# One full-array product for two 64x64 ones in the chunked recurrence of a hybrid backbone

## The chip, the cores and the metric

The kernel runs on one core of a Trainium2 chip. The metric is the device time of one execution in microseconds; the number to forecast is the median over several runs. TensorE appears in the profile as PE (the products) and PEld (the loads of the stationary operand, which overlap PE), VectorE as DVE, ScalarE as ACT, GpSimd as POOL, and the engine that issues the transfers as SP.

## The reference

Two layers over 1024 latent tokens and 256 context tokens, width 1024, all in float32. Each layer mixes tokens with three head groups (a gated MLP, a windowed attention, and an RWKV-7 recurrence of 4 heads of 64, run forwards and backwards), then applies a SwiGLU. What matters here is the recurrence:

```
def update(S, w_t, k_t, v_t, kk_t, a_t):
    sa = jnp.einsum('bhvk,bhk->bhv', S, kk_t)
    return (S * w_t[:, :, None, :] - sa[..., None] * (kk_t * a_t)[:, :, None, :]
            + v_t[..., None] * k_t[:, :, None, :])
def step(S, x):
    S = update(S, *x[1:])
    return S, jnp.einsum('bhvk,bhk->bhv', S, x[0])
```

## The kernel before

The recurrence is computed by chunks of 64 tokens. A chain is one direction and one pair of heads: 4 chains, 5 groups of 4 chunks each, so 80 units (`ul`) per layer and 160 in the kernel. The two heads of a pair lie on partitions 0 to 63 and 64 to 127. For every chunk the inverse of a 64x64 triangular matrix is made beforehand and kept in DRAM (`tb`), the two heads' inverses one below the other.

A unit passes through four stages. `u0` forms two masked 128x128 products. `u1` multiplies each head's inverse (`Ti`, 64x64) by that head's half of `t`. `u4` makes two 128x128 products, one for each head. `u5` updates the state (a 128x64 stationary operand per head, tile `u`) and makes the output (tile `uy`). The loop over n calls, for each n, u5 of unit n-4, u0 of unit n, u4 of unit n-2 and u1 of unit n-1, and then some background work: the output stage `rw_out` of chains that have ended (tile `gg`), and loads and splits of coming weights. The order in which TensorE gets the instructions is set when the program is compiled, and it isn't always that of the code. Every float32 product appears in the trace as two loads and two matmuls; so a stage with two products shows four of each. All of them carry L147, the line of the helper `mm`, and are told apart by tiles: u0 reads `u<-bC,bC`, u1 `u<-U,bC`, u4 `u<-bC`, u5 `u<-bC,U`, the output `uy<-U,bC`.

Three sets of four SBUF slots (`CH`) hold the operands of a group by turns (group number modulo 3). `chunk_set` zeroes and fills what stays constant in them. `beta_load` issues the loads of a group two groups ahead: two of `AB` (L1187), `KR` (L1189), `Ti` (L1190), the values `ZV` (L1196). `Ti` and `ZV` lie in a slot of their own (`C3`), taken afresh for each group. PSUM has two banks for u0, two for u4 and one each for u1, u5, uy and the background.

Of the kernel before, what the change touches and what calls it, by code (L numbers as in the profile page):

```python
# [93 lines left out]
def trunk(ctx: ExitStack, tc: tile.TileContext, x, ctxt, cc, w_mod, pp, w_in, w_out, lng, lnb, sgw, sink,  # L94
          w2, a2, g2, w_gu, w_down, cst, rope, out, dbg=None):
    nc = tc.nc
    V, S, G, T, D = nc.vector, nc.scalar, nc.gpsimd, nc.tensor, nc.sync
# [14 lines left out]
    def alloc(name, dt=F32):  # L112
        i = free.popleft()
        return Slot(sp.tile([128, NTOK], dt, tag=f"s{i}", name=nm(name)), i)
# [14 lines left out]
    def p_t(tag, bufs, n=512):  # L129
        return psum["pool"].tile([128, n], F32, tag=tag, name=nm(tag), bufs=bufs)  # L130
# [15 lines left out]
    def mm(o, lhsT, rhs, start=True, stop=True, parts=False):  # L146
        T.matmul(o, lhsT=lhsT, rhs=rhs, start=start, stop=stop, skip_group_check=parts)  # L147
# [42 lines left out]
    def bg(n, lane=0):  # L190
        q = (bgq, elq)[lane]
        owed[lane] += n
        while owed[lane] >= 1 and q:
            try:
                owed[lane] -= next(q[0]) or 1
            except StopIteration:
                q.popleft()
        if not q:
            owed[lane] = 0.0
# [96 lines left out]
    AB = [cp.tile([128, 4, 16], F32, name=f"ab{l}") for l in range(L)]  # L296
# [236 lines left out]
    def layer(l):  # L533
# [28 lines left out]
        tb = dr.tile([4, 128, NTOK], F32, name=f"tb{l}")  # L562
# [316 lines left out]
        for name in ("v", "u"):  # L879
# [3 lines left out]
            for t0 in range(0 if full else 2, NT, 2):  # L883
# [10 lines left out]
                for j in range(2):  # L894
                    t = t0 + j
# [248 lines left out]
        CH = []  # L1144

        def chunk_set():

            CH.append([alloc("bC") for _ in range(4)])  # L1150
            (V if CS else G).memset(CH[-1][2].t[:, 0:1024], 0.0)
            yield
            G.tensor_copy(CH[-1][3].t[:, 512:576], I2)
            for z in range(2):
                hp = slice(64 * z, 64 * z + 64)
                cv = CH[-1][z].t[hp, 0:1024].rearrange("p (c w) -> p c w", w=128)
                if CS > z:
                    S.activation(cv[:, :, 64:128], I2[hp].unsqueeze(1).to_broadcast([64, 8, 64]), AF.Copy)
                else:
                    G.tensor_copy(cv[:, :, 64:128], I2[hp].unsqueeze(1).to_broadcast([64, 8, 64]))  # L1160
                yield
# [9 lines left out]
        def beta_load(ci, gi):  # L1171

            d, pair = chains[ci]
            while ("join", ci) not in rw:
                bg(1, 1)
            H0, H1, AB, KR = (z.t[:, 0:1024] for z in CH[gl.index((ci, gi)) % 3])
            C3 = alloc("bC3")
            noY = gi == 0 and not full
            ZV, Ti = C3.t[:, 0:512], C3.t[:, 512:768]
            grp[ci, gi] = dict(c0=64 if noY else 0, H=(H0, H1), AB=AB, KR=KR, Ti=Ti, pc=(ci * 5 + gi) * 4, ZV=ZV, sl=C3)  # L1180
            src = cb[ci, gi]

            def c8(ap, q):
                return ap.rearrange("p (c q) -> p c q", q=q)
            for h in range(2):
                hp = slice(64 * h, 64 * h + 64)
                D.dma_start(c8(AB[hp], 128)[:, :, 64 - 64 * h:128 - 64 * h], c8(src[hp, 0:512], 64))  # L1187
            nw = 1 if noY else 2
            D.dma_start(KR[:, 0:256 * nw], src[:, 512:512 + 256 * nw])  # L1189
            D.dma_start(Ti, tb[ci][:, gi * 256:(gi + 1) * 256])  # L1190
            for h, H in enumerate((H0, H1)):
                hp = slice(64 * h, 64 * h + 64)
                later.append((H[hp].rearrange("p (c w q) -> p w c q", w=2, q=128)[:, 0:nw, :, 0:64],
                              KR[hp, 0:256 * nw].rearrange("p (w c t) -> p w c t", w=nw, t=64)))
            vs = vt[d, gi * 256:gi * 256 + 256, pair * 128:(pair + 1) * 128]
            D.dma_start(ZV[0:64].rearrange("p (c f) -> p c f", f=128), vs.rearrange("(c t) f -> t c f", t=64))  # L1196
            if gi == 0:
                G.memset(ZV[64:128, 0:128], 0.0)


        def unit(ci, gi, c):
            m = (ci * 20 + gi * 4 + c) % (2 * len(UR))
            g = grp[ci, gi]
            return g, UR[m // 2].t[:, m % 2 * 640:m % 2 * 640 + 512], g["c0"], [z[:, c * 256:c * 256 + 256] for z in g["H"]]
# [16 lines left out]
        def u1(ci, gi, c):  # L1221
            g, t, c0, C = unit(ci, gi, c)
            p = p_t("u1", PB["u1"])
            for h in range(2):
                hp = slice(64 * h, 64 * h + 64)
                mm(p[hp, c0:128], g["Ti"][hp, c * 64:c * 64 + 64], t[hp, c0:128])
            for h in range(2):
                oh = slice(64 - 64 * h, 128 - 64 * h)
                S.activation(C[h][oh, 128 + c0:256], p[oh, c0:128], AF.Copy)
# [93 lines left out]
        ul = [(ci, gi, c) for ci in range(4) for gi in range(5) for c in range(4)]  # L1323
        gl = [(ci, gi) for ci in range(4) for gi in range(5)]
        stages = {0: u0, 1: u1, 4: u4, 5: u5}

        def beta_start():
            yield from chunk_set()
            beta_load(*gl[0])
            yield  # L1330
            yield from chunk_set()
            own()
            beta_load(*gl[1])
            for _ in range(4):
                yield
            own()
# [27 lines left out]
        ps_open(True)  # L1364
        rw["beta"] = True
        run(chunk_set())
        UR = [alloc("U") for _ in range(NU)]
        GB = {}
        for n in range(len(ul) + max(s[1] for s in LG)):
            if n % 4 == LD and n // 4 + 2 < len(gl):  # L1370
                beta_load(*gl[n // 4 + 2])
            if n % 4 == (LD + OL) % 4:
                own()
            for s, lag in LG:
                m = n - lag
                if 0 <= m < len(ul):
                    ci, gi, c = ul[m]
                    stages[s](ci, gi, c)
                    if s == 5 and chains[ci][0] == 1 and c == 3 and gi in (0, 2, 4) and (full or gi):
                        bgq.append(rw_out(chains[ci][1], {0: 0, 2: 2, 4: 1}[gi]))  # L1380
            if n >= len(ul) - 24 and n % 4 == 1 and len(ready) < WR:
                emit_w(len(ready) >= 1)
            if n == len(ul) - 12 or (full and n == len(ul) - 9):
                GB[len(GB)] = gb_tile(l, 0, len(GB))
            if n < len(ul) + 2:
                bg(2 if n >= len(ul) - 8 else 1)
            bg(EL_B, 1)
# [576 lines left out]
```

## Time and profile before

| | |
|---|---|
| median of 3 runs | 3276.86 us (3274.75 to 3278.19) |
| profiled execution | 3271.0 us, of which the span from first to last instruction is 3269.2 us |
| PE busy | 3153.1 us (96%) |
| DVE, ACT, POOL busy | 62%, 41%, 16% of the span |
| stretches with the recurrence | 590 to 780 us (first layer), 2285 to 2480 us (second layer) |

Busy time is the time in which an engine has an instruction in work; the ends of matmuls are modelled, so neighbouring matmuls overlap in it. How long a product holds TensorE is better read from the starts of the loads: from the first load of one product to the first load of the next. In a timeline a row stands for several instructions of one kind in a row (x4), with the start of the first and the time until the last has ended.

### The profile page before, as it was taken

The page shows a single profiled execution, that of the slowest core. Times are in us where ns is not written, and L with a number is a line of the kernel's source. Part 1 is how long each engine was busy: PE and PEld are TensorE (multiplying, and loading weights), DVE is VectorE, ACT ScalarE, POOL GpSimd, SP SyncE. Part 2 cuts the span into 40 slices and gives each one's busy share as a digit, 9 for nine tenths or more (in the row PEclk, how much of TensorE's full clock was granted, in tenths as well). Part 3 has the DMA queues.
Part 4 walks back from the last instruction along what each step waited for, and adds up shares of the span by engine and source line. Part 5 has one row for each costly group of instructions (what it writes and reads, how often), then busy time and mean ns, then how long its engine had stood idle before and what let it go on. Part 6 is the DMA issues. An engine that isn't in the chain of part 4 may idle for free.

```text
span 3269.2 us, 51898 instructions
## 1 busy us (share of the span) xinstructions
PE 3153.1 (96%) x19892; PEld 2568.1 (79%) x19892; DVE 2038.0 (62%) x3978; ACT 1349.4 (41%) x2805; POOL 538.5 (16%) x616
## 2 busy tenths in 40 slices
PE   7998999999999999999999998999999999999998
PEld 4777978777788888886688777877777788888887
DVE  3458869676475555554455657779676666666556
ACT  4354477665342222222112544377665433333211
POOL 2103101232112222210001203101122122231000
PEclk8898999999999999999999999999999999999999
DMA  5684321445621212235722375412445222223322
GB/s 216 213 263 145 103 59 55 128 132 193 210 67 59 73 63 71 71 114 201 268 86 78 105 237 173 139 56 79 120 127 200 85 78 78 91 78 135 96 104 97
DMA packets 395176, 403.96 MB, mean 124 GB/s; under 512 B 113456, under 2 KB 334640, under 8 KB 394928
## 3 DMA queue, kind: packets, MB, share of 16 engines
q1 hardware_dynamic: 394928, 400.64, 37.8%
q8 instruction: 157, 2.57, 0.3%
q14 instruction: 91, 0.75, 0.1%
HBM read 279.97 MB, written 120.59 MB: 123 GB/s over the span
## 4 chain that ended last, share of the span: by engine, by line
PE 80%; DVE 8%; DMA 3%; issue 3%; ACT 3%; POOL 2%; SPq 1%; DVEq 0%; POOLq 0%; ACTq 0%
PE dd L147 26%; PE mm L147 24%; PE xx L147 18%; PE u L147 7%; PE mm L1118 1%; DMA wraw<-in_w_mod 1%; PE gg L147 1%; PE uy L147 1%; PE xx L1118 1%; DVE eX L666 1%; DVE eL L664 1%; DVE P L1071 1%; POOL ss L179 0%; DMA wm<-in_w_mod 0%; DVE yac L1697 0%
## 5 line engine op out<-in xcount | busy, mean ns | idle before, releaser
L147 PE MATMUL mm<-h,wh 128*128 128x512 f32 (+1 forms) x1424 | 424.2, 382 | 2.9 <-ACT ntmp L399 2.3
L147 PE MATMUL mm<-wh,h 128*128 128x256 f32 x1472 | 327.3, 299 | 0.5 <-DVE rtmp L946 0.5
L147 PE MATMUL dd<-h,wh 128*128 128x256 f32 (+1 forms) x1312 | 321.8, 336 | 1.5 <-DVE h L407 1.0
L147 PEld LDWEIGHTS mm<-h,wh 128*128 128x128 f32 x1424 | 261.8, 193 | 59.4 <-issue 10.0
L147 PE MATMUL mm<-h,wl 128*128 128x512 f32 (+1 forms) x712 | 268.5, 377 | 1.1 <-DVE wl L232 1.1
L147 PEld LDWEIGHTS mm<-wh,h 128*128 128x128 f32 x1472 | 252.1, 197 | 16.9 <-issue 15.8
L147 PEld LDWEIGHTS dd<-h,wh 128*128 128x128 f32 x1312 | 228.0, 191 | 29.2 <-DVE h L407 1.2
L1575 ACT ACTIVATE wh<-wq 128x1024 fp32r<-128x1024 f32 x114 | 121.0, 1061 | 302.8 <-PE dd L147 113.9
L147 PE MATMUL dd<-h,wl 128*128 128x256 f32 (+1 forms) x656 | 219.3, 334 | 0.0
L147 PE MATMUL mm<-wl,h 128*128 128x256 f32 x736 | 213.2, 290 | 4.3 <-DVE wl L232 4.3
L1576 DVE TENSOR_TENSOR wl<-wq,wh 128x1024 fp32r<-128x1024 f32 x114 | 141.1, 1238 | 114.8 <-ACT wh L1575 114.8
L179 POOL TENSOR_TENSOR ss<-ss,mh_sb 128x1 f32<-128x1 f32 x74 | 50.5, 683 | 838.2 <-DVE ss L376 836.0
L147 PE MATMUL dd<-tt,wh 128*128 128x512 f32 x608 | 188.1, 391 | 0.0
L147 PEld LDWEIGHTS mm<-h,wl 128*128 128x128 f32 x712 | 136.8, 192 | 25.3 <-DVE wl L232 1.4
L1697 DVE TENSOR_TENSOR yac<-yac,mm 128x512 f32<-128x512 f32 x126 | 86.4, 686 | 109.2 <-PE mm L147 109.2
L147 PEld LDWEIGHTS mm<-wl,h 128*128 128x128 f32 x736 | 145.0, 197 | 7.4 <-DVE wl L232 4.7
L1697 DVE TENSOR_TENSOR yac<-yac,xx 128x512 f32<-128x512 f32 x126 | 86.3, 685 | 91.8 <-PE xx L147 91.7
L1565 POOL TENSOR_TENSOR wq<-wu 128x512 f32<-128x512 f32 x38 | 49.1, 1292 | 561.8 <-DVE wl L1576 477.8
L147 PEld LDWEIGHTS dd<-h,wl 128*128 128x128 f32 x656 | 124.9, 190 | 12.4
L147 PEld LDWEIGHTS dd<-tt,wh 128*128 128x128 f32 x608 | 111.7, 188 | 21.3
L147 PE MATMUL u<-bC,bC 128*128 128x128 f32 (+1 forms) x640 | 118.3, 303 | 0.3 <-DVE bC L1219 0.3
L147 PE MATMUL dd<-tt,wl 128*128 128x512 f32 x304 | 118.3, 389 | 0.0
(370 smaller groups left out, 7769.7 us busy)
## 6 DMA issues: line engine op xcount, KB each, us to landing
wm<-in_w_mod SPq DMA_DIRECT2D x80, 512.0 KB, 5.2
wr<-in_w_down SPq DMA_DIRECT2D x44, 512.0 KB, 4.6
wr<-in_w_in SPq DMA_DIRECT2D x38, 512.0 KB, 4.4
cb<-ao SPq DMA_DIRECT2D x76, 256.0 KB, 2.7
wu<-in_w_gu SPq DMA_DIRECT2D x38, 512.0 KB, 3.7
wq<-in_w_gu SPq DMA_DIRECT2D x38, 512.0 KB, 3.7
ao<-rk SPq DMA_DIRECT2D x58, 256.0 KB, 4.0
xs<-xr SPq DMA_DIRECT2D x28, 512.0 KB, 2.7
```

What stands on the lines that cost most here:

```text
L147: T.matmul(o, lhsT=lhsT, rhs=rhs, start=start, stop=stop, skip_group_check=parts)
L179: G.tensor_tensor(dst, src, mh[:, :n], op=ALU.pow)
L664: V.tensor_tensor(tmp, Lm[:, j + 1:, j:j + 1].to_broadcast([n, r, c]), X[:, j:j + 1, :c].to_broadcast([n, r, c]), op=ALU.mult)
L666: V.tensor_tensor(X[:, j + 1:, :c], X[:, j + 1:, :c], tmp, op=ALU.subtract)
L1071: V.tensor_tensor_reduce(out=po, in0=pi, in1=m, scale=1.0, scalar=-3.0e38, op0=ALU.add, op1=ALU.max, accum_out=mx[:, h:h + 1])
L1118: T.transpose(ps[:, z * 128:(z + 1) * 128], P[i // 2].t[:, c:c + 128], ident)
L1565: G.tensor_tensor(a[:, 0:512], u[:, 0:512], u[:, 512:1024], op=ALU.add)
L1575: S.activation(w.hi[i], raw[i], AF.Copy)
L1576: V.tensor_tensor(w.lo[i], raw[i], f32(w.hi[i]), op=ALU.subtract)
L1697: V.tensor_tensor(yac[t].t[:, c], yac[t].t[:, c], ps, op=ALU.add)
```

## The change

The two heads' inverses are put on the diagonal of a 128x128 square that is zero elsewhere. `Ti` moves from `C3` into free columns (640 to 1151) of the fourth slot of the group's set in `CH`, which `chunk_set` zeroes once. The loads of `Ti` write only the two diagonal blocks, in two transfers, one for each head, instead of one. `u1` is then one product over all 128 rows and columns instead of two with 64x64.

```diff
             G.tensor_copy(CH[-1][3].t[:, 512:576], I2)
+            G.memset(CH[-1][3].t[:, 640:1152], 0.0)
...
-            H0, H1, AB, KR = (z.t[:, 0:1024] for z in CH[gl.index((ci, gi)) % 3])
+            cset = CH[gl.index((ci, gi)) % 3]
+            H0, H1, AB, KR = (z.t[:, 0:1024] for z in cset)
             C3 = alloc("bC3")
             noY = gi == 0 and not full
-            ZV, Ti = C3.t[:, 0:512], C3.t[:, 512:768]
+            ZV, Ti = C3.t[:, 0:512], cset[3].t[:, 640:1152]
...
-            D.dma_start(Ti, tb[ci][:, gi * 256:(gi + 1) * 256])
+            for h in range(2):
+                hp = slice(64 * h, 64 * h + 64)
+                D.dma_start(c8(Ti[hp], 128)[:, :, 64 * h:64 * h + 64], c8(tb[ci][hp, gi * 256:(gi + 1) * 256], 64))
...
             p = p_t("u1", PB["u1"])
-            for h in range(2):
-                hp = slice(64 * h, 64 * h + 64)
-                mm(p[hp, c0:128], g["Ti"][hp, c * 64:c * 64 + 64], t[hp, c0:128])
+            mm(p[:, c0:128], g["Ti"][:, c * 128:c * 128 + 128], t[:, c0:128])
```

## Rows read from the trace of the kernel before

**Rows 1.** The page: busy time of the engines; shares of the chain that ended last.
```profile
PE 3153.1 (96%) x19892; PEld 2568.1 (79%) x19892; DVE 2038.0 (62%) x3978; ACT 1349.4 (41%) x2805; POOL 538.5 (16%) x616
PE 80%; DVE 8%; DMA 3%; issue 3%; ACT 3%; POOL 2%; SPq 1%; DVEq 0%; POOLq 0%; ACTq 0%
```
**Rows 2.** Windows: window, length, busy PE PEld DVE ACT POOL, clock, DMA share, GB/s.
```profile
590.00:780.00 190.00, 185.21 (x1866) 139.60 (x1863) 138.39 (x451) 132.22 (x454) 54.19 (x66) 1.00 0.49 144
2285.00:2480.00 195.00, 186.73 (x1826) 142.74 (x1825) 133.83 (x439) 130.27 (x444) 45.10 (x61) 0.99 0.45 130
```
**Rows 3.** Waits of PE, longest in each stretch: us in total, times, longest.
```profile
PE mm L147 <- POOL Y L1275: 1.3, 1, 1.3
...
PE mm L1118 <- ACT P L1093: 2.5, 2, 2.2
```
**Rows 4.** Timeline of weight loads, 612 to 614 us: one unit in program order.
```profile
612.18 0.52 PEld L147 LDWEIGHTS u<-bC,bC 128*128 128x128 f32 x4
612.62 0.53 PEld L147 LDWEIGHTS u<-bC 128*128 128x128 f32 x4
613.27 0.20 PEld L147 LDWEIGHTS u<-U,bC 64*64 64x64 f32 x4
613.63 0.20 PEld L147 LDWEIGHTS u<-bC,U 128*64 128x64 f32 x4 [0.17 <-issue]
...
614.02 0.52 PEld L147 LDWEIGHTS u<-bC,bC 128*128 128x128 f32 x4
```
**Rows 5.** Timeline of weight loads, 702 to 705 us: one unit in another order.
```profile
702.39 0.19 PEld L147 LDWEIGHTS u<-U,bC 64*64 64x64 f32 x4
702.76 0.30 PEld L147 LDWEIGHTS u<-bC,bC 128*128 128x128 f32 x2 [0.17 <-issue]
703.17 0.19 PEld L147 LDWEIGHTS uy<-U,bC 128*64 128x64 f32 x2
703.43 0.30 PEld L147 LDWEIGHTS u<-bC,bC 128*128 128x128 f32 x2
703.85 0.20 PEld L147 LDWEIGHTS u<-bC,U 128*64 128x64 f32 x4
...
704.23 0.52 PEld L147 LDWEIGHTS u<-bC 128*128 128x128 f32 x4
704.88 0.20 PEld L147 LDWEIGHTS u<-U,bC 64*64 64x64 f32 x4
```
**Rows 6.** Instructions of tile u, those of u1: ns min/median/max, first and last start, forms.
```profile
L147 PEld LDWEIGHTS u<-U,bC x640: 129/130/133, 592.7 to 2472.2; 64*64 64x64 f32 x160
L147 PE MATMUL u<-U,bC x640: 218/269/320, 592.7 to 2472.3; 64*64 64x128 f32 x144, 64*64 64x64 f32 x16
```
**Rows 7.** Windows, instructions on tile u alone: busy PE, PEld, DVE, ACT.
```profile
590.00:780.00 190.00, 150.28 (x1264) 110.53 (x1264) 107.74 (x396) 88.06 (x316) 1.00 0.49 144
```
**Rows 8.** Transfers of a group: issue ns by line, landing us, and SP's longest wait.
```profile
L1190 SPq DMA_DIRECT2D bC<-tb x40: 319/382/943, 513.5 to 2443.9; - x40
L1187 SPq DMA_DIRECT2D bC<-cb x80: 573/625/821, 563.7 to 2442.5; - x80
bC<-cb SPq DMA_DIRECT2D x84, 128.0 KB, 2.8
SPq L1187 <- PE u L147: 73.7, 15, 8.5
```
**Rows 9.** GpSimd's memset at line 544: ns min/median/max, first and last start.
```profile
L544 POOL MEMSET lora<- x2: 951/952/954, 24.2 to 1823.9; 128x1024 f32 x2
```
**Rows 10.** The chain in order of time, end of the first layer's recurrence.
```profile
770.79 0.27 ACT bC L1229
...
771.52 0.84 ACT mhi L1413
```

## The prediction

> **What bounds the kernel now.** I began with the page. PE is busy for 96% of the span and carries 80% of the chain that ended last [rows 1]; so time taken off TensorE should come off the end, unless another engine bounds the stretch in question. The change touches the recurrence alone, and I read its two stretches next. In both PE is busy for 186 to 187 us, where DVE and ACT have 130 to 138 us, and the granted clock is 1.00 and 0.99, the upper of its two levels (2.4 GHz) [rows 2]. PE hardly waits: the longest entry of its waits is 1.3 us in the first stretch and 2.5 us in the second [rows 3], and all of them together are 4.5 us (5 rows) and 7.5 us (11 rows). DVE has 107.74 us and ACT 88.06 us of work for the 80 units' tile u, 1.35 and 1.10 us a unit [rows 7], against at least 1.84 us in which a unit passes through PE [rows 4]. So the reader should look for what a unit costs on PE.
>
> The starts of the loads tell that. In [rows 4] the eight loads of u0 and u4 follow each other by 0.11 us (0.44 us for four). After u4's last load, though, 0.32 us go by until u1's first: u4 takes 0.65 us where its four loads alone explain 0.44. The shape changes there, from 128x128 to 64x64. The same extra stands in [rows 5] at the change to 128x64: the second half of u0, two loads, holds PE for 0.42 us (703.43 to 703.85), so 0.31 us from last load to next. I take 0.31 us for a step at which the shape changes away from 128x128, against 0.11 us where it stays. PE's "waits" don't show this time.
>
> **What the change removes and adds on PE.** Now u1 has four loads of 64x64, in pairs side by side, and the next product's first load comes 0.36 to 0.37 us after u1's first (613.27 to 613.63, 702.39 to 702.76). From u4's last load over u1 to whatever follows is thus 0.31 + 0.37 = 0.68 us. With the change u1 has two loads of 128x128 and no change of shape behind u4. No row shows such a u1, but u0 and u4 are the same instruction in form.
> - Where a 128x64 product follows (u5 or uy, as in [rows 4]), the three steps become 0.11 + 0.11 + 0.31 = 0.53 us: 0.15 us saved. The switch isn't lost, it moves behind u1.
> - Where a 128x128 product follows (half of u0 as in [rows 5], or background gg), they become 3 x 0.11 = 0.33 us: 0.35 us saved, because two switches go.
>
> The trace has 640 loads of u1 [rows 6], four for each of 160 units. By walking through all of them in the loads' timeline I count 84 of the first kind and 64 of the second; a dozen have other neighbours, or loads missing from the record, and I give them nothing. Sum: 84 x 0.15 + 64 x 0.35 = 12.6 + 22.4 = 35 us. Sixteen units have only 64 moving columns (the second form of the matmuls in [rows 6]); u1 is cheaper there already, and I take off 2 us as an estimate. That is the upper end with the order kept: 33 us.
>
> Then what isn't bound by PE. In the last stretch of each recurrence the chain runs through ACT, with u1's evacuation beside splits of the output stage [rows 10], about six units a layer. Twelve units at the mean saving of 0.22 us are 2.6 us that I strike, and 2.4 us more for places where PE's existing short waits [rows 3] grow because PE arrives earlier. 33 - 5 = 28 us.
>
> **What covers the rest.** *The second transfer.* Each of 40 groups gets two strided issues instead of one. They have the form of AB's, 0.625 us each against 0.382 us for Ti now [rows 8]: 2 x 0.625 - 0.382 = 0.87 us of SP a group, 35 us in all. SP has that time: it stands 73.7 us in the first layer at L1187 alone, waiting for PE to be through with a set [rows 8]. Behind Ti stand ZV and the background's loads. If the cover were gone, a group would start 0.87 us late, up to 35 us; I take nothing, for the reason that follows. *A new wait.* Ti now overwrites columns that u1 of three groups back still reads, so its issue waits for the last u1 of that group, with ZV behind it on SP. AB already waits for the u0 of the same unit, which PE passes one unit earlier, 1.84 to 2.49 us [rows 4, 5]; two issues of AB and one of KR, at 0.6 us each [rows 8], take up 1.8 us of that, so SP stops for another 0 to 1 us. Between that u1 and the first that reads the new Ti lie eight units, at least 8 x 1.84 = 14.7 us, and a load lands in 2.8 us [rows 8]; so below it is nothing, and above, with 1 us on each of 34 groups and no slack, 34 us. I take nothing. *The memsets.* Six on GpSimd, half the width of one that takes 0.952 us [rows 9], so at most 0.95 us and nearer 0.5; POOL is busy for 54 of 190 us [rows 2], and the first u1 that reads them comes later. The third set's could hold u0's operands up by 1 us a layer; I take nothing and keep 2 us for the range. *Evacuation.* L1229 reads the same PSUM tile as before. u1's first load comes 0.20 us sooner (0.31 - 0.11), its last one 0.11 us behind that, so the result isn't later and I charge nothing.
>
> Against the profiled execution of 3271.0 us (3269.2 us of span and 1.8 us around it) 28 us less is 3243.0 us. It lies 5.9 us below the median of the runs, so I forecast 3276.9 - 28 = 3249 us.
>
> **A rule that speaks against it.** The rows show that u1's two products run side by side: four loads of 0.13 us each end 0.19 to 0.20 us after the first began [rows 4, 5, 6]. Without the 0.20 us that the switch adds (0.31 - 0.11) a u1 costs 0.37 - 0.20 = 0.17 us now; a full one costs 2 x 0.11 = 0.22 us. Taken alone the product gets dearer by 0.05 us. The Trainium skill ("TensorE: Matmul & The Clock Gate", Part 3, on packing small matmuls) says just that: products of 64 rows and columns in separate quarters of the array run at the same time, and that is the remedy for small ones; the change undoes it. By that rule alone the kernel would be slower. The rows around u1 decide otherwise, because they show the switch as well, and the trace agrees with the packing but not with its being the cheaper form here.
>
> **The rivals.**
> 1. *Order gets worse* (other side). PE's order is set at compile time: the code has u5, uy, u0, u4, u1, yet [rows 5] have u0 split around uy. A unit in program order takes 1.84 us (612.18 to 614.02), one in the order of [rows 5] takes 2.49 us (702.39 to 704.88). With the change they take 1.69 and 2.14 us. Fewer products in u1 may make the planner place u0 and uy elsewhere. Each unit that goes from the first order to the second costs 0.45 us: at 62 units the 28 us are gone, at 90 units the time is 3276.9 + 12 = 3289 us. For it: 47 of the units already stand with u0 or uy split, by my count in the loads' timeline, and small things decide. Against it: the work to be ordered and the lags are the same.
> 2. *Order gets better*: the same in reverse, or more units with u0 next to u1. With two switches gone everywhere, 150 x 0.35 = 52 us, 3225 us.
> 3. *The switch stays*, and the pairs side by side were free: u1 lands between 128x64 products, or the step isn't one of shape at all. 160 x 0.05 = 8 us more, 3285 us. Against it: u0 to u4 has no such step.
> 4. *ACT becomes the bound*: a unit's ACT work with the output's evacuation and splits is near 1.3 us on average, 132.22 us in 190 us [rows 2], and comes in order. If half the savings fall on its waits, 14 us remain: 3263 us.
>
> **How the numbers follow.** Forecast 0.53 (3241 to 3257); worse order 0.15, of which 0.03 stay faster, 0.05 end level and 0.07 slower; better order 0.14; the switch stays 0.05, slower; ACT binds 0.13, of which 0.02 end level. A measurement can tell about 0.2%, 6.6 us, from no change. Faster: 0.53 + 0.03 + 0.14 + 0.11 = 0.81; same 0.07; slower 0.12. The range goes from the better order's 3225 up to a gain just lost, 3279: what is left out is the slower cases above it, 0.12, and little below.
>
> **What will show it.** Right: 320 loads of 128x128 for u1 in place of 640; 0.11 us between u4's last load and u1's first; 0.31 us from u1's last load to a u5; a unit in program order of about 1.69 us; recurrence stretches some 14 us shorter each, the rest unchanged. Wrong: more units with u0 split around uy; PE waits for L1229 or L1254 in the stretches; u1 at a group's start waiting for the transfer of tb; or a step of 0.3 us that still stands ahead of u1.

## The result and the profile after

The changed kernel takes 3299.52 us (median of 4 runs, 3297.27 to 3301.01) against 3277.51 us of the kernel before (4 runs of its own on the same chip): ratio 1.0068, 95% interval 1.0056 to 1.0080. It is 22 us slower where 28 us less was forecast, outside the range of 3225 to 3279. The profiled execution took 3301.01 us.

What the prediction said of the products themselves came true. The instructions on tile `u` (count, then ns min/median/max, first and last start, forms) answer to [rows 6]: half as many loads, all of them full.

```profile
L147 PEld LDWEIGHTS u<-U,bC x320: 186/192/333, 593.3 to 2498.8; 128*128 128x128 f32 x160
L147 PE MATMUL u<-U,bC x320: 222/275/421, 593.4 to 2498.9; 128*128 128x128 f32 x144, 128*128 128x64 f32 x16
```

The timeline of weight loads from 603.6 to 605.6 us (start, length, engine, line) shows a unit in program order, as [rows 4] did.

```profile
603.65 0.30 PEld L147 LDWEIGHTS u<-U,bC 128*128 128x128 f32 x2
604.07 0.20 PEld L147 LDWEIGHTS u<-bC,U 128*64 128x64 f32 x4
604.18 0.20 PEld L147 LDWEIGHTS uy<-U,bC 128*64 128x64 f32 x4
604.45 0.52 PEld L147 LDWEIGHTS u<-bC,bC 128*128 128x128 f32 x4
604.89 0.53 PEld L147 LDWEIGHTS u<-bC 128*128 128x128 f32 x4
605.34 0.30 PEld L147 LDWEIGHTS u<-U,bC 128*128 128x128 f32 x2
```

From one u1 to the next are 1.69 us (603.65 to 605.34), the very number forecast. u4's four loads and the step to u1 take 0.45 us instead of 0.65; the 0.42 us from u1 to u5 are 0.11 + 0.31, so the switch of shape has moved behind u1.

Yet the stretches got longer. From the first to the last load of the recurrence's products the first takes 190.4 us (591.5 to 781.9; before 183.0, 590.6 to 773.6), the second 187.0 us (2317.9 to 2505.0; before 179.4, 2298.7 to 2478.1). The page's line of busy time and its shares of the chain, for [rows 1] (this chain goes back over less than a third of the span, so its shares can't be set beside those of before):

```profile
PE 3160.0 (96%) x19572; PEld 2590.7 (79%) x19572; DVE 2037.4 (62%) x3978; ACT 1350.4 (41%) x2805; POOL 541.1 (16%) x622
PE 26%; issue 1%; DVE 1%; ACT 1%; POOL 0%; DMA 0%; POOLq 0%; DVEq 0%; ACTq 0%
```

Windows over the two stretches, columns as in [rows 2], and PE's longest waits from 590 to 795 us, as in [rows 3] (L1256 and L1231 are L1254 and L1229 of before; the two waits of tile `dd` lie behind the stretch):

```profile
590.00:780.00 190.00, 179.99 (x1690) 147.13 (x1685) 129.47 (x437) 123.53 (x437) 51.42 (x64) 0.99 0.45 127
2300.00:2510.00 210.00, 191.24 (x1721) 154.71 (x1720) 139.47 (x452) 133.76 (x453) 46.62 (x62) 0.96 0.43 119
```

```profile
PE u L147 <- ACT bC L1256: 2.8, 5, 1.2
PE dd L147 <- DVE mlo L1416: 1.7, 1, 1.7
PE dd L147 <- ACT mhi L1415: 1.5, 1, 1.5
PE uy L147 <- ACT Yb L1269: 1.4, 1, 1.4
PE u L147 <- ACT bC L1231: 1.2, 3, 0.7
```

PE is now idle for 10.0 us of the first window (190.00 - 179.99), where it was for 4.8. No single wait explains it. What does is seen in the timeline of weight loads a little later, over four units from the u1 at 617.79 to that at 626.04 us:

```profile
617.79 0.30 PEld L147 LDWEIGHTS u<-U,bC 128*128 128x128 f32 x2
618.01 0.68 PEld L147 LDWEIGHTS u<-bC,bC 128*128 128x128 f32 x4
...
619.22 0.30 PEld L147 LDWEIGHTS u<-U,bC 128*128 128x128 f32 x2
...
620.02 0.30 PEld L147 LDWEIGHTS u<-bC,bC 128*128 128x128 f32 x2
...
620.69 0.30 PEld L147 LDWEIGHTS u<-U,bC 128*128 128x128 f32 x2
...
622.13 0.30 PEld L147 LDWEIGHTS u<-U,bC 128*128 128x128 f32 x2
...
623.07 0.59 PEld L147 LDWEIGHTS u<-bC 128*128 128x128 f32 x4 [0.19 <-ACT bC L1231]
623.78 0.19 PEld L147 LDWEIGHTS uy<-U,bC 128*64 128x64 f32 x2
624.04 0.97 PEld L147 LDWEIGHTS u<-bC,bC 128*128 128x128 f32 x8
625.13 0.20 PEld L147 LDWEIGHTS u<-bC,U 128*64 128x64 f32 x4
625.24 0.20 PEld L147 LDWEIGHTS uy<-U,bC 128*64 128x64 f32 x2
625.82 0.30 PEld L147 LDWEIGHTS u<-bC,bC 128*128 128x128 f32 x2 [0.38 <-PE uy L147]
626.04 0.30 PEld L147 LDWEIGHTS u<-U,bC 128*128 128x128 f32 x2
```

Three units of 1.43 to 1.47 us are followed by one of 3.91 us: 8.25 us for four, 2.06 each, where the units of [rows 4] took 1.84. In the long one stand ten loads of u0, eight of them in a row, those of two units; u5 and uy are in pieces around them, and PE waits for ACT or for its own last result (0.19 and 0.38 us). The units behind such a knot have less of u0 left to do: four loads, two and none in the three shown. More than four loads of u0 in a row, with no other product of the recurrence between them, stand at 25 places in the two stretches, where before had 5; two of them, the starts of the stretches, are in every kernel here. From u1 to u1 over both layers (158 intervals): the median fell from 1.91 to 1.70 us, but intervals over 3 us went from 11 to 28, and the mean rose from 2.21 to 2.28 us.

I priced each step between two load starts at the lower fifth of its kind (tiles and shapes of both loads) over the sixteen kernels here; what a step takes beyond that is excess (waits and dependent products). Over the two stretches the standard steps went from 319 to 296 us, 24 less where the forecast has 33; the excess went from 43 to 82 us. The split depends somewhat on how the kinds are drawn, so it is an estimate; the sums, 362 and 377 us, are the stretches.

A second part of the loss stands at the end of the first recurrence, where no `u` is left. There the loads `os<-od` of the stage that follows the recurrence (second row) are issued on SP at 778.31 us, behind transfers of the background and weight loads; before, one was out at 756.16 us and the next followed from 766.38 us on. The timeline of SP after:

```profile
773.75 0.91 SPq L223 DMA_DIRECT2D wr<-in_w_out  x2
778.31 1.30 SPq L1408 DMA_DIRECT2D os<-od  x3
```

and the timeline of PE's products, with what each waited for:

```profile
787.39 0.50 PE L147 MATMUL dd<-wh,mhi 128*128 128x512 f32 x1 [1.48 <-ACT mhi L1415]
...
789.83 0.79 PE L147 MATMUL dd<-wh,mlo 128*128 128x512 f32 x1 [1.70 <-DVE mlo L1416]
790.42 0.63 PE L147 MATMUL dd<-wh,mhi 128*128 128x512 f32 x1
```

and windows of 5 us there, first of after, then of before:

```profile
775.00:780.00 5.00, 4.88 (x24) 2.30 (x24) 2.45 (x8) 2.58 (x7) 2.31 (x2) 0.66 0.93 321
780.00:785.00 5.00, 3.30 (x13) 1.18 (x14) 4.11 (x9) 3.51 (x9) 3.08 (x3) 0.68 0.61 222
785.00:790.00 5.00, 1.81 (x5) 0.47 (x4) 4.05 (x5) 3.81 (x5) 0.00 (x0) 0.84 0.24 67
790.00:795.00 5.00, 5.00 (x12) 3.93 (x13) 2.74 (x3) 2.12 (x4) 0.00 (x0) 0.50 0.87 305
```

```profile
771.00:776.00 5.00, 2.63 (x25) 1.26 (x24) 4.48 (x7) 4.85 (x14) 1.65 (x2) 1.00 0.59 193
776.00:781.00 5.00, 4.45 (x17) 3.06 (x18) 5.00 (x7) 3.22 (x6) 0.12 (x1) 1.00 0.97 317
```

The granted clock of after is down for parts of the windows from 775 us on, and from 790 to 795 us, behind a window in which PE works for 1.81 us of five, it is 0.50, the lower of the two levels (1.2 GHz). The kernel before had 1.00 in the four windows of 5 us from 766 to 786 us, also where PE worked for 2.63 us of five, so these rows don't say what tips it.

Set beside each other instruction by instruction, after is 1.1 us late at 550 us, 14.3 at 800, 17.3 ahead of the second recurrence and 29.8 behind it, in the two profiled executions, which stand 30.0 us apart. Part of that is time at the lower level: the mean granted clock of the two executions is 0.976 against 0.981, which makes 2 x (0.024 x 3299 - 0.019 x 3269) = 34 us more of it. With the same products 0.43 us apart at that level and 0.23 us at the upper one (last section), it is worth up to 16 of the 30 us, as an estimate.

### The profile page after: what moved, and what is told of

Its sections match the earlier page's. It is cut to its first block, busy times and chain, and to the rows that moved or that the text cites. A ratio compares the mean times of both kernels' runs of the same rounds, so it can differ in the third digit from the quotient of the medians.

```text
span 3299.2 us, 51485 instructions
## 1 busy us (share of the span) xinstructions
PE 3160.0 (96%) x19572; PEld 2590.7 (79%) x19572; DVE 2037.4 (62%) x3978; ACT 1350.4 (41%) x2805; POOL 541.1 (16%) x622
```

## The experiments

Times are medians; a ratio is to the kernel before, run on the same chip beside it, with its 95% interval. Before took 3276.72, 3275.70, 3277.71 and 3276.85 us in the four sets of runs. "Rows out of order" counts, in the listing of TensorE's compiled instructions, rows of the recurrence's products that stand behind a product which the code issues later: 67 for before, 210 for after. It is no time, but it can be compared. The traces bear it out: counted in the same manner over the starts of the loads, with u5 and uy taken as one, 80 stand so in before and 192 in after (7 and 69 of them u0's), and none in a kernel with all five stages chained.

**The order fixed, in both kernels.** Order-only edges (no wait on the chip) chain u0, u1, u4, u5 and uy in the order in which the code issues them:

```
-        T.matmul(o, lhsT=lhsT, rhs=rhs, start=start, stop=stop, skip_group_check=parts)
+        i = T.matmul(o, lhsT=lhsT, rhs=rhs, start=start, stop=stop, skip_group_check=parts)
+        if chain:
+            if chain[0] is not None:
+                tc.add_manual_dep(i.ins, chain[0].ins.name, NOSYNC, reason="order")
+            chain[0] = i
...
+                    chain.append(last_u[0])
                     stages[s](ci, gi, c)
+                    last_u[0] = chain.pop()
```

The change with the chain:

> The changed kernel, with TensorE's products of the recurrence (u0, u1, u4, u5, uy) held to the order of the code by order-only edges; nothing else differs. Theory A (the compile-time order is at fault: it makes TensorE meet products whose inputs aren't there): with the regular order the stalls of the two recurrences, 83 us in the changed kernel against 40 us before, go back to about 40 us or less, and the 32 us saved in the steps remain: 3277 - 32 - some 8 us for fewer changes of shape = about 3237 us, and a steady unit of 1.70 us. Theory B (the stalls belong to the full product: with less work on TensorE the other engines' latencies show, whatever the order): the stalls stay near 80 us, 3285 to 3300 us, and steady units stay above 1.84 us. Theory C (the loads of the inverses come late): u1 at the start of a group waits for them in this order too, 3280 us or more.

The kernel before with the chain:

> The kernel before with the same order-only edges; the two 64x64 products stay. It parts what the order gives from what the product gives. Theory A: 480 changes of shape instead of 524 by the compiled order, at 0.2 us each, so some 9 us less than before, about 3268 us, and the changed kernel in order lies 0.15 us x 150 = 22 to 32 us below it. Theory B: the same gain for the order, but the changed kernel in order isn't below it. If the order were worth nothing either way: 3277 us.

The change in order takes 3268.54 us, ratio 0.9975 [0.9966, 0.9985]: 31 us less than the change without the chain and faster than before. Before in order is level, 3274.40 us, 0.9997 [0.9987, 1.0006]. So the order of the products is what turned a gain into a loss, and before had little to win from it. The mean granted clock isn't what the chain gives back: by the medians of the runs it is 0.976 with it and 0.976 to 0.977 without. In order, the change is still only 6 us ahead of before, where about 3237 us had been expected of it.

**The parts of the change alone.** The loads alone: memset, square and two transfers as in the change, but two products that read the diagonal blocks.

```
-                mm(p[hp, c0:128], g["Ti"][hp, c * 64:c * 64 + 64], t[hp, c0:128])
+                mm(p[hp, c0:128], g["Ti"][hp, c * 128 + 64 * h:c * 128 + 64 * h + 64], t[hp, c0:128])
```

> The changed kernel with the two 64x64 products put back, reading the diagonal blocks of the square: the new place, the two transfers and the memsets without the full product; order free. Theory C (the loads, their wait for the u1 of three groups back, and the memsets cost the time): as slow as the changed kernel, about 3299 us. Theory A and B (the product's smaller share of TensorE's time): near the kernel before, 3277 us, give or take 8 us for an order with 534 changes of shape instead of 524.

It takes 3336.49 us, 1.0185 [1.0168, 1.0202], 214 rows out of order: the loads, which the prediction costed at nothing, lose 60 us by themselves, and the product then wins 37 us back. The product in a square of the group's own, with a memset per group:

```
-            G.memset(CH[-1][3].t[:, 640:1152], 0.0)
...
-            ZV, Ti = C3.t[:, 0:512], cset[3].t[:, 640:1152]
+            ZV, Ti = C3.t[:, 0:512], C3.t[:, 512:1024]
+            G.memset(Ti, 0.0)
```

> The full product with its square in the group's own slot, zeroed anew for each group on GpSimd (40 memsets of 128x512), so that no load waits for a u1 of three groups back; order free. Theory C: the time of the changed kernel goes, and the saving of some 28 us shows, about 3250 us. Theory A and B: as slow as the changed kernel, 3290 to 3305 us; its compiled order has 354 changes of shape against 352.

It takes 3290.59 us, 1.0048 [1.0033, 1.0063], 162 rows out of order. No wait for an old u1 is left there, but the two strided transfers are, and it is still slower than before.

**Another way to fill the square.** `tb` is loaded in one contiguous transfer into `C3` again, and GpSimd copies the blocks onto the diagonal, with the copies that it makes for `H` anyway:

```
-            for h in range(2):
-                hp = slice(64 * h, 64 * h + 64)
-                D.dma_start(c8(Ti[hp], 128)[:, :, 64 * h:64 * h + 64], c8(tb[ci][hp, gi * 256:(gi + 1) * 256], 64))
+            TC = C3.t[:, 512:768]
+            D.dma_start(TC, tb[ci][:, gi * 256:(gi + 1) * 256])
+            for h in range(2):
+                hp = slice(64 * h, 64 * h + 64)
+                later.append((c8(Ti[hp], 128)[:, :, 64 * h:64 * h + 64], c8(TC[hp], 64)))
```

> The full product as in the change, but tb is loaded as before, in one contiguous transfer into C3, and GpSimd copies the two heads' blocks from there into the square's diagonal (two more 64x256 copies a group, beside those it makes already for u4). Order theory (the two strided transfers make the compiled order of the products worse, and that order is what the change pays for): the compiled order now has 71 rows of the recurrence's products behind a later one's, about before's 67 and not the change's 210, with the change's 352 switches of shape; so the standard steps' saving of 32 us stays and the excess is near before's 40 us: 3245 to 3262 us. Theory that the full product itself costs the time, by waits that a faster TensorE only makes visible: as the change in order, 3265 to 3272 us, or above. Theory that GpSimd's copies come too late: u4 or u1 wait for them, over 3280 us.

The same with the chain:

> The kernel with the square filled by GpSimd's copies, with the recurrence's products chained in the order of the code besides. If code order is the best one, 0 to 10 us faster than the same kernel without the chain; if some of the compiled order's moves fill waits (u5 or half of u0 put where a product would wait), 0 to 10 us slower. Beside the change in order (3268.5 us) it has no strided transfer and no wait of the loads for u1: about the same if those cost nothing once order is kept, 5 to 15 us faster if they cost.

Both beat both kernels: 3261.13 us, 0.9956 [0.9941, 0.9971], without the chain (71 rows out of order), and 3253.94 us, 0.9935 [0.9916, 0.9954], with it; the two intervals overlap. The second is 5 us from the 3249 us forecast for the change, and 45 us below the change. Its timeline of weight loads, two units:

```profile
611.89 0.30 PEld L150 LDWEIGHTS u<-U,bC 128*128 128x128 f32 x2
...
613.58 0.30 PEld L150 LDWEIGHTS u<-U,bC 128*128 128x128 f32 x2
...
615.27 0.30 PEld L150 LDWEIGHTS u<-U,bC 128*128 128x128 f32 x2
```

1.69 us a unit, kept up here; its stretches last 174.4 and 161.6 us instead of before's 183.0 and 179.4, 26 us less. Without the chain they last 171.4 and 170.3 us. The copies cost GpSimd little, by the row of their line in the kernel without the chain (ns min/median/max):

```profile
L1169 POOL COPY bC<-bC x160: 389/400/1782, 560.0 to 2436.7; 64x256 f32<-64x256 f32 x88, 64x512 f32<-64x512 f32 x72
```

Some 80 more copies of 0.4 us each.

**What in the loads does it.** Five kernels with two 64x64 products: both halves of the new loads with the chain, then four with one half each. The loads of the change with the chain:

> The two 64x64 products kept, the loads as in the change (two strided transfers into the square of three groups), products chained in the order of the code. Order theory: as the kernel before in order, 3274 us, within 6 us, although the same loads without the chain gave 3336 us. Theory that the transfers or the wait for u1 cost time on the chip: 3290 to 3335 us, with u1 or u0 waiting on a transfer at the groups' starts.

Strided transfers into the group's own buffer, no old u1 to wait for, no chain:

```
-            ZV, Ti = C3.t[:, 0:512], C3.t[:, 512:768]
+            ZV, Ti = C3.t[:, 0:512], C3.t[:, 512:1024]
...
+                D.dma_start(c8(Ti[hp], 128)[:, :, 64 * h:64 * h + 64], c8(tb[ci][hp, gi * 256:(gi + 1) * 256], 64))
```

> The two 64x64 products kept; the two strided transfers go into C3, a buffer of the group's own, so nothing waits for an old u1; no memset, and only the diagonal blocks are read. Products not chained. Its compiled order has 155 rows behind a later one's (before 67, the loads of the change alone 214). Order theory by form of transfer: between before and the loads alone, 3295 to 3325 us. Theory that the wait for the old u1 is the cause: near before, 3275 to 3283 us.

The same with the chain:

> The two 64x64 products kept and chained in the order of the code; the two strided transfers of the change go into the group's own buffer, so no issue waits for an old u1. If the form of the transfers (twice the issues, elements of 256 bytes) is the cause of the 16 us: 3284 to 3292 us. If the wait is: 3271 to 3278 us. Halves for both: 3278 to 3284 us.

One contiguous transfer into the three-group set, so that the wait for the old u1 is there alone, with the chain and without:

```
-            ZV, Ti = C3.t[:, 0:512], C3.t[:, 512:768]
+            ZV, Ti = C3.t[:, 0:512], cset[3].t[:, 640:896]
```

> The two 64x64 products kept and chained in the order of the code; tb is loaded in one contiguous transfer as before, but into 256 of the columns of the three-group set that the change uses, so that its issue waits for the u1 of three groups back, and the issues behind it on SP with it. The loads of the change in order cost about 16 us over before in order (3290.7 against 3274.4). If the wait, with what stands behind it on SP, is the cause: 3284 to 3292 us. If the strided transfers are: 3271 to 3278 us.

> The two 64x64 products, tb in one contiguous transfer into the three-group set, not chained: the wait for the old u1 alone. Its compiled order has 65 rows out of the code's order, as before's 67. Order theory by form of transfer: level with before, 3272 to 3282 us. If the wait alone costs what the loads together cost without a chain (60 us, 40 of them seen with strided transfers and no wait): 3290 to 3300 us.

The loads of the change in order took 3290.73 us, 16 us more than before in order (14 by the ratios), so the order of the recurrence's products isn't the whole of their price. Strided transfers into the group's own buffer took 3316.12 us without the chain and 3286.98 us with it, both as expected if the form of the transfers is the cause; the wait for the old u1 took 3276.55 us in order, as expected if it is not, and 3286.93 us without the chain, which neither theory has.

All ratios together, with the rows out of order where nothing is chained:

```
loads of Ti                          two 64x64, no chain       two 64x64, chain         full product, no chain    full product, chain
contiguous, into C3                  1 (67 rows)               0.9997 [.9987, 1.0006]   0.9956 [.9941, .9971] *   0.9935 [.9916, .9954] *
contiguous, wait for old u1          1.0033 [1.0016, 1.0051]   0.9995 [.9982, 1.0008]   -                         -
                                     (65 rows)
strided, own buffer                  1.0124 [1.0107, 1.0141]   1.0028 [1.0013, 1.0043]  1.0048 [1.0033, 1.0063] + -
                                     (155 rows)
strided, wait for old u1             1.0185 [1.0168, 1.0202]   1.0040 [1.0024, 1.0056]  1.0068 [1.0056, 1.0080]   0.9975 [.9966, .9985]
                                     (214 rows)                                         (210 rows)
* with GpSimd's copies (71 rows without the chain)    + with a memset for each group (162 rows)
```

In order the wait costs nothing that can be measured (0.9995 against 0.9997). The strided form costs 10 us (1.0028 - 0.9997 = 0.0031 of 3277), and 41 us without the chain. The wait alone without the chain came out at 11 us against an expected level; its profiled run has stretches as long as before's (183.0 and 179.8 us), and its rows out of order are before's. Its runs reach from 3278.93 to 3301.40 us, and they go by the granted clock: 0.979 in the two fastest, 0.973, 0.973 and 0.972 in the three slowest, where before had 0.979 in the middle. Its median is 0.9765, which makes 2 x 0.0025 x 3287 = 16 us more at the lower level; by the rows 0.43 and 0.23 us apart (last section) that is worth up to 8 of the 11 us, as an estimate. What lowers the clock in some of its runs isn't shown.

The heaps of u0 in the traces follow the form of the transfers. Places with more than four u0 loads in a row are 30 (loads alone), 25 (the change), 20 (the product in its own square) and 19 (strided, own buffer) where the transfers are strided and nothing is chained; 5 (before), 4 (copies) and 6 (the wait alone) where they are contiguous; and 2, the starts of the stretches, wherever u0 is chained.

On the chip a strided transfer is not late. In after's DMA view of 590 to 770 us (KB each, median us to landing) and in the row of its issues:

```profile
bC<-tb SPq DMA_DIRECT2D x36, 64.0 KB, 2.6
```

```profile
L1194 SPq DMA_DIRECT2D bC<-tb x80: 573/580/1674, 557.5 to 2469.8; - x80
```

Before's single one landed in 3.1 us in the same window. Nor is an operand late: from the landing of a group's `tb` to the first load of u1 that reads it there are at least 3.8 us in after (median 18.6; before 14.1 and 20.1), from the landing of its `cb` to u0 at least 2.2 us (before 5.5); in the kernel with strided transfers into the own buffer, in order, 13.5 and 2.0 us. SP's waits in after from 590 to 795 us (total, times, longest) say the same; it still waits longest for u0, as in [rows 8], and the issues of `tb` wait 12.9 us in 16 times:

```profile
SPq L1189 <- PE u L147: 61.2, 16, 7.1
...
SPq L1194 <- PE uy L147: 7.3, 11, 1.2
SPq L1194 <- PE u L147: 5.6, 5, 1.8
```

So what the strided form does is done for the most part before the kernel runs: the compiled order puts a unit's u0 later and in one heap with the next unit's, as if its operands came late. That the compiler reckons strided transfers dearer than they are is the likeliest reading, but no run shows its reckoning.

**Which part of the order matters, and the rest that is left.** With the copies, only u0, u4 and u1 chained (u5 and uy free), which leaves 49 rows out of order, 45 of them u5 or uy:

> The kernel with the square filled by GpSimd's copies; only u0, u4 and u1 are chained in the order of the code, u5 and uy may be put anywhere by the compiler. Without a chain this kernel took 3261.1 us (71 rows out of the code's order, 14 of them u0's), with all five chained 3253.9 us. If what hurts is u0 put late, near the fully chained one: 3250 to 3256 us. If u5 and uy out of order cost as well: 3257 to 3262 us.

3258.62 us, 0.9942 [0.9920, 0.9964]: between the two, and not told apart from either, so it doesn't decide. Then every product of the loop chained, the background's too, in the change and in the kernel with copies:

> The change with its strided transfers; every product that the recurrence's loop issues, the background's included, is chained in the order of the code, not the recurrence's alone. With the recurrence's chained it took 3268.5 us, 14.6 us more than the same with the square filled by GpSimd's copies (3253.9 us). If that rest comes from where the compiler puts the background's products (gg) among the others, it is gone: within 5 us of the next kernel. If the strided transfers cost it on the chip, or through the other engines' orders, 10 to 18 us above the next kernel.

> The kernel with the square filled by GpSimd's copies, every product of the loop chained in the order of the code, the background's too; its order on TensorE differs from that of the last kernel in 54 lines of the listing (the two with the recurrence alone chained differ in 135). If code order suits the background as well, 3250 to 3258 us; if its products then stand before their inputs are there, 3260 to 3275 us.

3270.86 us, 0.9974 [0.9960, 0.9988], and 3263.00 us, 0.9959 [0.9941, 0.9978]. The difference is 8 us by the medians (5 by the ratios) where it was 15, and the intervals overlap: neither expectation is met. For the background's products code order is no better than the compiler's: with the copies it was rather worse (3253.94 us with the recurrence's alone), though these intervals overlap too.

Where the strided form's last 10 us lie can be read from the traces. Against before in order, the kernel with strided transfers into the own buffer in order loses 3.8 us in the first stretch (185.8 against 182.0), 3.7 us right behind it and 4.7 us in the second stretch (177.3 against 172.6). Behind the first stretch SP's order differs: in each of the eight kernels with strided transfers the first load of `os` is issued 3.4 to 4.1 us before the recurrence's last load, in each of the eight with a contiguous one 17 to 25 us before it, whether TensorE's products are chained or not. What is lost there is 3.5 to 3.9 us in three pairs in the code's order and 0.9 us in the pair with all products chained. So a part of the 10 us goes with the order of SP's issues, which no edge here holds. Whether the part in the stretches is the order of the background's products, the other engines' orders or the chip stays open. For the first speak PE's waits from 640 to 760 us in the loads-alone kernel in order, the longest of which are background products:

```profile
PE gg L150 <- DVE gsx L1314: 1.9, 2, 1.3
PE gg L150 <- ACT gvg L1316: 1.6, 1, 1.6
PE gg L150 <- DVE Y L1328: 1.4, 2, 0.8
```

In the kernel before in order no gg product waits for these there; its longest entry is u5's result from ACT, 2.1 us.

## Why the prediction was wrong

*The steps between loads: right.* 0.11 us from u4's last load to u1's first, the switch behind u1, 1.69 us for a unit in program order; the standard steps shrank by 24 us against 33 to 35 forecast. The rival that the switch stays is out. The Trainium skill ("TensorE: Matmul & The Clock Gate", Part 3) names several small products at the same time in separate parts of the array as the remedy for small ones. The runs speak against that as the rule that decides here: with the loads left contiguous the full product is worth 14 us without the chain (0.9956) and 20 us with it (0.9935 against 0.9997).

*"The work to be ordered and the lags are the same": the step that failed.* The first rival, a worse order, came true, and I gave it 0.15 because I had looked for its cause only in u1's fewer products. I costed the loads' new form by what it does to a running chip (0.87 us of SP a group, hidden) and there it was right: SP had the time, and nothing landed late. But the order that the compiler makes changes with the form of the transfers. The same loads with the old products lose 60 us without the chain and 13 to 14 us with it. I priced the rival itself right in kind, by units in the order of [rows 5], yet its true form was another: u0 of two units together, a knot of about 4 us at some 17 units more (intervals over 3 us: 11 to 28). Two of the signs that I had named came with it: pairs of u0's loads that stand apart from their other half went from 40 to 60, and PE's waits for L1229 and L1254 (now L1231 and L1256) in the first stretch from 1.7 to 4.0 us.

*"A new wait, nothing":* right in order (0.9995 against 0.9997). Without the chain 11 us were measured, in runs whose granted clock is lower the longer they are.

*The memsets and the evacuation at nothing:* no wait of PE names a memset. PE's waits for u1's evacuation (L1229, now L1231) are 1.2 us in after's first stretch against 0.9, so little came of it there. No run has either alone.

*ACT as the bound:* ACT's evacuations are the first of PE's waits (2.8 us at L1256), but the kernel with copies in order shows that most of the 28 us was to be had: its stretches are 26 us shorter, although excess there rose from 43 to 56 us, so a third of the saving in steps (from 319 to 280 us) goes to waits: more than the 5 us that I struck, but of that kind. That it comes so near the forecast is in part luck. The 39 us of steps are more than the 33 forecast, because 15 of them come from the order of the code alone (304 us in before in order), and the 13 us of waits make up for it.

*"The rest unchanged": wrong.* The order on SP changed too, and the end of the first recurrence lost its early loads and the upper clock level. Of the 13.2 us that after falls behind from 550 to 800 us, 7.4 lie in the longer stretch (190.4 - 183.0) and 5.8 behind it.

## What to carry over

Where a compiler orders the instructions of a kernel, the form of a transfer can cost time in two ways: on the chip, read from landing times and queue waits, and through the order that is compiled around it; the second shows in the compiled listing and in the order of the load starts, and no wait has its name. A gain per instruction that shows in the load starts, and a total that gets worse, call for fixing the order by edges in both kernels first: here that separated 31 us of order from the rest. And zero borders that need strided loads can be had by a contiguous load and a copy on an idle engine.

## What the runs showed of the hardware beyond that

A strided 64 KB transfer in 256-byte elements landed in 2.6 us and a contiguous one of 128 KB in 3.1 us, while the packets under 512 bytes in the window from 590 to 770 us rose from 21976 to 31949. At equal size, `AB`'s 128 KB in 256-byte elements landed in 2.8 us in before's same window:

```profile
bC<-cb SPq DMA_DIRECT2D x36, 128.0 KB, 2.8
bC<-tb SPq DMA_DIRECT2D x17, 128.0 KB, 3.1
```

The Trainium skill ("DMA: Bandwidth & Descriptors", Specifications) gives 512 bytes as the least size for the full rate. At these sizes that shows in no transfer's landing; no run here has transfers large enough to read a full rate from.

From 790 to 795 us after's PE was busy throughout at a granted clock of 0.50, where the same products' rows are 0.43 us apart; at the upper level, after 795.5 us, they are 0.23 us apart.
